# Loading the first tile of a rotary-embedding kernel in halves on two queues, with the tables behind one half

## The chip, the cores and the metric

The kernel runs on one core of a Trainium2 chip. Its time is the device time of one execution in microseconds, as the median of several; the span of a profile is shorter by some 1.4 us (161.19 against 159.8 in the profiled run of the kernel before). Runs of the kernel before agree within about 0.5%; a few runs come out some per cent slower, and comparisons leave those out.

## The reference

`x` is 16 x 512 x 1024 in float32, that is 33.6 MB in and as much out. Each row of 1024 is 16 heads of 64, and each head is rotated by tables that depend on the position alone:

```
x1, x2 = x[..., :32], x[..., 32:]                 # per head
rotated = concatenate([x1*cos - x2*sin, x1*sin + x2*cos])
```

`cos` and `sin` are 512 x 32 each: 64 KB, and so each about a thousandth of the bytes moved.

## The kernel before

The data are cut into 10 tiles. Tiles 0, 1, 8 and 9 hold one batch (4 rows of 1024 per partition, 2 MB); the six between hold two batches (8 rows, 4 MB). They live in a ring of 40 rows, so the first six tiles can be loaded at once; the other four are loaded when stores have freed their place. For each of the 64 rows VectorE writes x times cosine to PSUM, and GpSimd writes the swapped x times the signed sine to one of six buffers in SBUF (six of the rows have this product on VectorE). The sum is made by VectorE for 43 rows, and for 21 by TensorE, which adds the second product into PSUM; ScalarE then copies the result back.

ScalarE issues all the loads, in one queue, with both tables behind tile 0. SyncE issues all the stores.

```python
def on_scalar(ae):
    later = {}
    for t, (b, n) in enumerate(tiles):
        if b * R1 + n <= RING:
            load(ae, t)                                # tiles 0 to 5
        else:
            later.setdefault(... + R2 - 1 + LAG, []).append(t)
        if t == 0:
            for i, (table, sem) in enumerate(((cos, sem_cos), (sin, sem_sin))):
                ae.dma_start(stage[:, i, :], table.rearrange("(s r) d -> s (r d)", r=R1)).then_inc(sem, 16)
    ae.wait_ge(sem_sin, 16)
    ...                                                # the signed sine tables
    for u in range(NU):
        if PE2[u]:                                     # TensorE's rows: copy the sum back
            ae.wait_ge(sem_e, n_pe[u])
            ae.activation(xs[:, u % RING, :], t1_ps[:, u % NT1, :], COPY).then_inc(sem_a, 1)
        for t in later.get(u, ()):                     # a reissued load waits for a store
            ...
            ae.wait_ge(sem_out[k], 16 * stores_of(k))
            load(ae, t)
```

GpSimd's program: it waits for the signed sine table before its first row (and for that of the larger tiles before tile 2, left out below), then per tile for its load, and per row for a free buffer.

```python
    for u in range(NU):
        ...
        if (t, r) == (0, 0):
            pl.wait_ge(sem_s, 1)
        ...
        pl.wait_ge(sem_in[t], 16)
        wait_t2_free(pl, u)
        pl.tensor_tensor(t2_sb[:, u % NT2, :, :, :], swapped(k), over_heads(s_of(t, r)), mult).then_inc(sem_p, 1)
```

## Time and profile before

| | before |
|---|---|
| time, median of 3 runs | 161.44 us |
| span of the profile | 159.8 us |
| bytes moved | 67.26 MB, at 421 GB/s over the span |
| DMA engines | busy from 1.83 us to 159.35 us |
| GpSimd | 58 products, 134.1 us busy, from 9.56 to 149.74 us |
| last add ends, last store issued | 151.06, 151.14 us |

Two things stand close to the end of this kernel: the bytes, and GpSimd. The prediction below shows the lines of the page. One more is needed here, from SyncE's own waits (columns: what waited for what, total in us, times, longest): the wait for the last store after it was issued.

```profile
SPq L162 <- DMA out_dram<-x_sb: 8.3, 1, 8.3
```

A store of 2 MB is 8 packets of 16 KB on each engine, of 0.611 us each in this trace, 4.9 us. That this one took 8.3 us from its issue shows that stores had piled up: the compute was finished before the queue was.

### The profile page before, as it was taken

What the parts mean: (1) busy time and instruction counts of PE and PEld (TensorE: products, weight loads), DVE (VectorE), ACT (ScalarE), POOL (GpSimd) and SP (SyncE); (2) the same over time, 40 slices, a digit from 0 to 9 for tenths busy, and PEclk for the clock granted to TensorE, in tenths of its full rate; (3) what the DMA queues carried; (4) which work ended last, traced back from release to release, by engine and by line L of the source; (5) the groups of instructions that cost most, each with busy time, mean ns of one, the idle gap of its engine ahead of it and who ended that gap; (6) DMA issues with size and microseconds to landing.
All of it is one profiled execution on the core that took longest, in us unless ns stands there. A gap on an engine that the chain in (4) does not pass through costs nothing.

```text
span 159.8 us, 568 instructions
## 1 busy us (share of the span) xinstructions
PE 70.9 (44%) x94; PEld 23.3 (15%) x94; DVE 130.6 (82%) x117; ACT 23.9 (15%) x26; POOL 136.4 (85%) x67
## 2 busy tenths in 40 slices
PE   6050005375437642680943409435848764950000
PEld 1020002021202210220211002110222121310000
DVE  0069998799999999987989729899989998989500
ACT  0320000205020502022012020222022202130000
POOL 5069999999999999999999999994999999289400
PEclk9999999959876995576598775995555555576555
DMA  5999999999999999999999999999999999999997
GB/s 144 395 458 480 394 394 431 422 509 410 394 427 427 494 418 402 451 459 404 402 468 443 394 459 451 402 435 418 418 439 472 435 402 418 492 402 435 390 447 304
DMA packets 3170, 67.26 MB, mean 421 GB/s; under 512 B 352, under 2 KB 608, under 8 KB 608
## 3 DMA queue, kind: packets, MB, share of 16 engines
q10 hardware_dynamic: 1728, 33.69, 49.8%
q1 hardware_dynamic: 1440, 33.56, 48.8%
q14 instruction: 2, 0.02, 0.0%
HBM read 33.69 MB, written 33.55 MB: 421 GB/s over the span
## 4 chain that ended last, share of the span: by engine, by line
DMA 30%; POOL 18%; issue 17%; DVE 17%; PE 8%; ACT 3%; ACTq 2%; POOLq 0%; DVEq 0%; SPq 0%
DMA out_dram<-x_sb 18%; POOL t_sb L265 18%; DMA x_sb<-in_x_dram 11%; DVE x_sb L312 8%; PE t_ps L220 8%; DVE t_ps L301 7%; ACT x_sb L186 3%; ACTq L153 1%; DVE t_sb L294 1%; ACTq L174 1%; POOLq L144 0%; POOLq L146 0%; DVEq L311 0%; DVEq L146 0%; SPq L137 0%
## 5 line engine op out<-in xcount | busy, mean ns | idle before, releaser
L265 POOL TENSOR_TENSOR t_sb<-x_sb,s_sb 128x1024 f32<-128x1024 f32 x58 | 134.1, 2363 | 12.5 <-ACT s_sb L178 6.5
L220 PE MATMUL t_ps<-t_sb,ident 128*128 128x512 f32 x84 | 66.1, 940 | 64.8 <-DVE t_ps L301 34.7
L301 DVE TENSOR_TENSOR t_ps<-x_sb,pair_ps 128x1024 f32<-128x1024 f32 x48 | 57.7, 1223 | 8.2 <-ACT x_sb L186 7.9
L312 DVE TENSOR_TENSOR x_sb<-t_ps,t_sb 128x1024 f32<-128x1024 f32 x43 | 52.4, 1220 | 2.7 <-POOL t_sb L265 2.6
L186 ACT ACTIVATE x_sb<-t_ps 128x1024 f32<-128x1024 f32 x21 | 21.5, 1023 | 109.8 <-PE t_ps L220 97.7
L220 PEld LDWEIGHTS t_ps<-t_sb,ident 128*128 128x128 f32 x84 | 21.4, 279 | 109.2 <-DVE t_ps L301 60.2
L301 DVE TENSOR_TENSOR t_ps<-x_sb,tab_ps 128x1024 f32<-128x1024 f32 x16 | 19.3, 1222 | 1.1 <-DMA x_sb<-in_x_dram 0.6
L294 DVE TENSOR_TENSOR t_sb<-x_sb,tab_ps 128x1024 f32<-128x1024 f32 x6 | 7.3, 1215 | 0.0
L272 DVE COPY tab_ps<-stage 128x128 f32<-128x128 f32 x1 | 0.3, 295 | 7.6 <-DMA stage<-in_cos_dram 7.6
L203 PE MATMUL pair_ps<-stage,pick 128*128 128x256 f32 x4 | 2.0, 668 | 5.1 <-DMA stage<-in_sin_dram 5.1
L196 PE MATMUL t_ps<-zero 128*128 128x512 bf16 x6 | 2.7, 630 | 1.3 <-DVE zero L270 1.3
L177 ACT ACT_TABLE_LOAD x1 | 1.3, 1283 | 5.4 <-issue 5.4
L203 PEld LDWEIGHTS pair_ps<-stage,pick 128*128 128x128 f32 x4 | 1.2, 326 | 6.1 <-issue 6.0
L246 POOL TENSOR_SCALAR_AFFINE_SELECT pick<-pick 128x128 f32<-128x128 f32 x2 | 1.4, 704 | 0.1
L196 PEld LDWEIGHTS t_ps<-zero 128*128 128x128 bf16 x6 | 0.7, 137 | 2.4 <-DVE zero L270 1.2
L270 DVE MEMSET zero<- 128x256 uint32 x1 | 0.3, 272 | 0.9 <-PEq L345 0.9
L177 ACT ACTIVATE s_sb<-stage 128x128 f32<-128x128 f32 x1 | 0.3, 310 | 2.3 <-DMA stage<-in_sin_dram 2.3
L181 ACT ACTIVATE s_sb<-pair_ps 128x256 f32<-128x256 f32 x1 | 0.4, 384 | 1.7 <-PE pair_ps L203 1.7
L231 POOL MEMSET ident<- 128x128 f32 x1 | 0.2, 205 | 0.3 <-POOLq L345 0.3
L182 ACT ACTIVATE s_sb<-pair_ps 128x256 f32<-128x256 f32 x1 | 0.4, 378 | 0.0
L233 POOL TENSOR_SCALAR_AFFINE_SELECT ident<-ident 128x128 f32<-128x128 f32 x1 | 0.3, 294 | 0.1
L345 POOL MEMSET const-float32-0.0<- 128x1 f32 x1 | 0.1, 98 | 0.3 <-issue 0.3
(7 smaller groups left out, 1.3 us busy)
## 6 DMA issues: line engine op xcount, KB each, us to landing
x_sb<-in_x_dram ACTq DMA_DIRECT2D x6, 4096.0 KB, 38.8
out_dram<-x_sb SPq DMA_DIRECT2D x6, 4096.0 KB, 25.7
x_sb<-in_x_dram ACTq DMA_DIRECT2D x4, 2048.0 KB, 22.7
out_dram<-x_sb SPq DMA_DIRECT2D x4, 2048.0 KB, 15.0
stage<-in_cos_dram ACTq DMA_DIRECT2D x1, 64.0 KB, 7.5
stage<-in_sin_dram ACTq DMA_DIRECT2D x1, 64.0 KB, 7.3
```

What stands on the lines that cost most here:

```text
L153: eng.dma_start(in_sbuf(t), in_dram(x1, x2, t)).then_inc(sem_in[t], 16)
L174: ae.dma_start(stage[:, i, :], table.rearrange("(s r) d -> s (r d)", r=R1)).then_inc(sem, 16)
L177: ae.activation(s1_sb[:, :, 0, :], sv, COPY, scale=-1.0)
L186: ae.activation(xs[:, u % RING, :], t1_ps[:, u % NT1, :], COPY).then_inc(sem_a, 1)
L196: pe.matmul(t1_ps[:, k, b * BANK:(b + 1) * BANK], zero[:, 0:P], zero[:], start=True, stop=True).then_inc(sem_w, 1)
L203: pe.matmul(pair_ps[:, k].rearrange("p c r d -> p (c r d)"), pick[:, k].rearrange("q s b -> q (s b)"), stage[:].rearrange("q c f -> q (c f)"),
L220: ins = pe.matmul(t1_ps[:, u % NT1, b * BANK:(b + 1) * BANK], ident[:], t2[:, b * BANK:(b + 1) * BANK], start=False, stop=True, skip_group ...
L246: pl.affine_select(out=pick[:, k], in_=pick[:, k], compare_op=mybir.AluOpType.is_equal, fill=0.0, base=-k, pattern=[[-2, P // 2], [0, 2]], ...
L265: pl.tensor_tensor(t2_sb[:, u % NT2, :, :, :], swapped(k), over_heads(s_of(t, r)), mult).then_inc(sem_p, 1)
L294: ve.tensor_tensor(t2_sb[:, u % NT2, :, :, :], swapped(k), over_heads(v_ps), mult)
L301: ve.tensor_tensor(t1_ps[:, u % NT1, :].rearrange("p (h d) -> p h d", d=HALF), x_sb[:, k, :, :, :].rearrange("p h t d -> p (h t) d"), c_of ...
L312: ve.tensor_tensor(xs[:, k, :], t1_ps[:, u % NT1, :], t2_sb[:, u % NT2, :, :, :].rearrange("p h t d -> p (h t d)"), add,).then_inc(sem_v, 1)
```

## The change

Two queues are to start at once, so that the first tile should be there sooner, and the tables should come right behind it without standing before tile 1. The core of the diff; the waits for tile 0 count 32 in place of 16, as the tile now has two DMAs with `then_inc(sem_in[0], 16)`:

```diff
+        def load_half(eng, i):
+            eng.dma_start(
+                x_sb[:, i * HR:(i + 1) * HR].rearrange("p n h t d -> p (n h t d)"),
+                x1[0, :, i * HR * dim:(i + 1) * HR * dim],
+            ).then_inc(sem_in[0], 16)
 ...
         def on_sync(sp):
+            load_half(sp, 0)
+            for i, (table, sem) in enumerate(((cos, sem_cos), (sin, sem_sin))):
+                sp.dma_start(stage[:, i, :], table.rearrange("(s r) d -> s (r d)", r=R1)).then_inc(sem, 16)
 ...
         def on_scalar(ae):
+            load_half(ae, 1)
             later = {}
             for t, (b, n) in enumerate(tiles):
+                if t == 0:
+                    continue
                 if b * R1 + n <= RING:
                     load(ae, t)
 ...
-                if t == 0:
-                    for i, (table, sem) in enumerate(((cos, sem_cos), (sin, sem_sin))):
-                        ae.dma_start(stage[:, i, :], ...).then_inc(sem, 16)
```

More of the change, by code (lines that the diff above doesn't have):

```diff
@@ L150, in stores_of @@
             return sum(b * R1 // R2 == k for b, _ in tiles)
+        HR = R1 // 2
+        def load_half(eng, i):
[3 more added lines that the diff above has]
+            ).then_inc(sem_in[0], 16)
         def load(eng, t):
@@ L171, in on_scalar @@
                     later.setdefault((b * R1 - RING) // R2 * R2 + R2 - 1 + LAG, []).append(t)
-                if t == 0:
-                    for i, (table, sem) in enumerate(((cos, sem_cos), (sin, sem_sin))):
-                        ae.dma_start(stage[:, i, :], table.rearrange("(s r) d -> s (r d)", r=R1)).then_inc(sem, 16)
             ae.wait_ge(sem_sin, 16)
@@ L262, in on_gpsimd @@
                     pl.wait_ge(sem_s, 2)
-                pl.wait_ge(sem_in[t], 16)
+                pl.wait_ge(sem_in[t], 32 if t == 0 else 16)
                 wait_t2_free(pl, u)
@@ L286, in mul @@
                 if r == 0:
-                    ve.wait_ge(sem_in[t], 16)
+                    ve.wait_ge(sem_in[t], 32 if t == 0 else 16)
                 if (t, r) == (2, 0):
```

## The prediction

> **What bounds the kernel now.** I read the page's slices first, then the queue totals, the groups, the windows, the chain, the timeline of the start, and last the single packets of the DMA record.
>
> ```profile
> span 159.8 us, 568 instructions
> ...
> DMA  5999999999999999999999999999999999999997
> ...
> DMA packets 3170, 67.26 MB, mean 421 GB/s; under 512 B 352, under 2 KB 608, under 8 KB 608
> ...
> q10 hardware_dynamic: 1728, 33.69, 49.8%
> q1 hardware_dynamic: 1440, 33.56, 48.8%
> ```
>
> The 16 DMA engines are busy from the first slice to the last. q10 is ScalarE's queue (all loads), q1 SyncE's (all stores). The packet record gives 611 ns for a 16 KB packet and 1213 ns for a 32 KB one on one engine, so 16 engines move 429 to 432 GB/s and 67.2 MB need about 156 us. The kernel is bound by its bytes. What stands beside them is GpSimd:
>
> ```profile
> L265 POOL TENSOR_TENSOR t_sb<-x_sb,s_sb 128x1024 f32<-128x1024 f32 x58 | 134.1, 2363 | 12.5 <-ACT s_sb L178 6.5
> ...
> L272 DVE COPY tab_ps<-stage 128x128 f32<-128x128 f32 x1 | 0.3, 295 | 7.6 <-DMA stage<-in_cos_dram 7.6
> ```
>
> 58 products occupy it 134.1 us, 2.31 us from one to the next. It is idle 12.5 us: 6.5 before the first, until the sine table is there, and 6.0 after. Of those 6.0, the waits give 5.8 to loads:
>
> ```profile
> POOL t_sb L265 <- ACT s_sb L178: 6.5, 1, 6.5
> POOL t_sb L265 <- DMA x_sb<-in_x_dram: 5.8, 2, 3.6
> ```
>
> So a later start of GpSimd is free only for about 6 us; after that GpSimd sets the end. The start, from the timeline:
>
> ```profile
> 1.21 0.46 ACTq L174 DMA_DIRECT2D stage<-in_cos_dram  x1
> 1.69 0.45 ACTq L174 DMA_DIRECT2D stage<-in_sin_dram  x1
> ...
> 8.97 0.31 ACT L177 ACTIVATE s_sb<-stage 128x128 f32<-128x128 f32 x1 [2.25 <-DMA stage<-in_sin_dram]
> ...
> 9.56 20.80 POOL L265 TENSOR_TENSOR t_sb<-x_sb,s_sb 128x1024 f32<-128x1024 f32 x9 [6.50 <-ACT s_sb L178]
> ```
>
> Sine lands just before 8.97, and 0.59 us later GpSimd starts. The end, from the chain in order of time and the windows (columns PE, PEld, DVE, ACT, POOL, clock, DMA share, GB/s):
>
> ```profile
> 149.84 1.23 DVE x_sb L312
> ```
>
> ```profile
> 150.00:160.00 10.00, 0.00 (x0) 0.00 (x0) 1.06 (x1) 0.00 (x0) 0.00 (x0) 0.50 0.88 377
> ```
>
> The last add ends at 151.07, its store is issued at 151.14, but its first packets run at 153.7 to 154.5, behind the previous store; the last packet ends at about 159.3. Compute has some 2.7 us of slack even there.
>
> [...] q1 and q10 together never exceed the rate of one alone. [...] From 24 us to 37.5 us one engine's packets run store 16 KB, load 32 KB, store 16 KB, load 32 KB, one of each, for all eight of a DMA, whatever their size. At 37.47 us even the 4-byte packets that end each DMA [...] take turns: load's 4 B, store's 4 B (6 ns later), load's 32 KB. So here a turn is one descriptor, however small. [...]
>
> **The change part by part.** (1) First tile in halves on two queues. Bytes are equal; both halves start with the first packet at about 1.83 us as before (ScalarE issues at 0.81, SyncE is free as early). An engine does 16 packets of 8 KB in turns in place of 8 of 16 KB; by the 16 KB and 32 KB times a packet costs some 9 ns beside its bytes, so 8 x 9 = 0.07 us more. Both halves land where the tile landed, about 7.65 to 7.9 us. Issue time saved is worth nothing, as the first packets come 1.0 us after the issue's start anyway. Worth: 0, at most 0.3 us either way.
>
> (2) Tables behind their half on SyncE's queue. Before, they stood in ScalarE's queue between tile 0 and tile 1; an engine did its 8 + 8 packets of 512 B in 16 x 27 ns = 0.43 us with nothing between. After, SyncE's ring holds 8 packets of cosine and 8 of sine, and ScalarE's ring holds tile 1 (8 x 16 KB per engine), then tile 2 (8 x 32 KB). One for one, cosine goes beside tile 1: 8 x (0.611 + 0.027) = 5.1 us. Sine goes beside tile 2: 8 x (1.213 + 0.027) = 9.9 us. So sine ends at 7.9 + 5.1 + 9.9 = 22.9 us, as tile 2 ends; in the trace of before tile 2 ends at 22.6 to 23.1, with the same bytes ahead of it, which checks the sum. With 0.45 us from last packet to the waiting engine, as before (8.53 to 8.97), and perhaps one 32 KB packet less if the table goes first in each pair: sine lands at 22.3 to 23.5, say 23.0, in place of 8.97. That is 14.0 us later.
>
> (3) What follows. GpSimd starts at 23.6 in place of 9.56. Loads run on meanwhile and fill the 40-row ring; DMA loses no time at first, but stores begin 14 us later, at about 34 us. GpSimd then should find its inputs there: the ring holds the first six tiles, and the later loads, reissued when stores land, come 14 us later than before at worst while their use is as much later. I count its two load waits (3.64 + 2.16) as gone. Its end: 149.75 + 14.0 - 5.8 = 157.95. The last add, 1.32 later: 159.3. Then the last store without a backlog: stores before it are done, since 4.9 us of the previous 2 MB fit into the 9 us between the two. Issue to first packet 1.0 us (0.81 to 1.83 above), 8 x 0.611 = 4.9, plus 0.3 for engines that start late and 0.45 from last packet to the end of the span: 159.35 + 1.0 + 4.9 + 0.3 + 0.45 = 166.0 us of span. Kernel time is 161.44 - 159.8 = 1.64 above the span: 167.6 us. The stores alone give the same bound: the next-to-last pair's store is issued at about 143 to 146, then 9.7 + 4.9 + 4.9 us of packets: 163.5 to 166.5.
>
> **The rivals.** *Tables land early.* If an engine takes all eight 512 B descriptors in one turn [...], the tables wait for two or three big packets and land at 9 to 11 us. GpSimd loses at most 2 us, the 6 us of waits absorb that, and the bytes set the end again: 161.0 to 161.8. Against it: the 4-byte packets that take single turns, and each 512 B descriptor a packet of its own in the record (608 packets under 2 KB = 352 + 256 table packets). Chance 0.13. *Late tables, and more lost behind.* With GpSimd never waiting, VectorE has 64 + 43 + 6 operations of 1.22 us less overlap, about 130 us, to fit beside its 134, and TensorE's adds in the windows run at a granted clock of 0.50 to 0.67. If they hold VectorE up, or the later stores delay the reissued loads, 1 to 3 us come on top: 168.5 to 170.5. For it: VectorE waits 8.3 us for ScalarE's copies of TensorE's sums now. Against it: GpSimd waited only 0.3 us for TensorE. Chance 0.2. *Partly late:* only cosine is late[...]: start 6 to 8 us later, 162.5 to 164.5. Chance 0.07. *Faster:* from halves landing sooner. The bytes forbid it: 0.01.
>
> **Range and chances.** 0.6 for the main sum at 165.5 to 168.5, 0.2 above it, 0.2 below. Predicted 167.6; 165.0 to 169.8 should hold it 8 times in 10. Slower by 2% begins at 164.7: faster 0.01, same 0.14, slower 0.85.
>
> **What would show it.** Right: GpSimd's idle before its first product near 20 us, with the sine table as releaser; the issue-to-landing time of cosine near 12 and of sine near 21 to 22 us against 7.5 and 7.3; no wait of GpSimd for loads later; DMA slices below 9 late in the span; 2.31 us per product unchanged. Wrong: tables landing before 12 us with the time at 161 (turns are not single descriptors), or tables landing at 23 and the time below 165 (more slack in GpSimd than the 6 us I counted), or GpSimd still waiting for loads.

The sum came to 166.0 us of span and 167.6 us of time. The record's "descriptor" is one packet of the trace (the page's 608 packets under 2 KB are 352 of 4 B and 256 of 512 B, the rows of the two tables), and its "ring" is the packets of one queue on one engine. That the two queues together are no faster than one is seen in the windows of the kernel before: 431 GB/s from 8 to 24 us with loads alone, 436 and 434 GB/s from 30 to 60 and from 60 to 100 us with loads and stores. The 0.3 us "for engines that start late" was an estimate; in the changed kernel the 16 engines started the last store within 0.15 us (161.035 to 161.186).

## The result, and the profile after

The changed kernel takes 167.66 us (median of 6 runs, 167.52 to 167.97), the kernel before in the same rounds 161.43 us. The ratio is 1.0391, with a 95% interval of 1.0377 to 1.0405. Here and below a ratio is the mean time of one kernel's fast runs over that of the other's in the same rounds, so it is not quite the ratio of the medians.

The issues and landings of the changed kernel (columns: what is written and read, engine, how many, size of each, us from issue to landing):

```profile
x_sb<-in_x_dram SPq DMA_DIRECT2D x1, 1024.0 KB, 7.4
x_sb<-in_x_dram ACTq DMA_DIRECT2D x1, 1024.0 KB, 8.4
stage<-in_cos_dram SPq DMA_DIRECT2D x1, 64.0 KB, 12.9
stage<-in_sin_dram SPq DMA_DIRECT2D x1, 64.0 KB, 22.4
```

Both tables took 7.3 to 7.5 us before. The sine table, 64 KB, now takes three times as long as half a tile of 1 MB. The timeline of the start shows who stands waiting, and the waits show what GpSimd waits for in the whole run:

```profile
14.20 0.29 DVE L284 COPY tab_ps<-stage 128x128 f32<-128x128 f32 x1 [13.00 <-DMA stage<-in_cos_dram]
...
24.14 0.31 ACT L189 ACTIVATE s_sb<-stage 128x128 f32<-128x128 f32 x1 [18.51 <-DMA stage<-in_sin_dram]
```

```profile
POOL t_sb L277 <- ACT s_sb L190: 21.6, 1, 21.6
```

```profile
L277 POOL TENSOR_TENSOR t_sb<-x_sb,s_sb 128x1024 f32<-128x1024 f32 x58 | 134.1, 2375 | 21.6 <-ACT s_sb L190 21.6
```

GpSimd starts at 24.73 us in place of 9.56 and then never waits again: its whole idle time, 21.6 us, is that one wait. The two waits for loads, 5.8 us before, are gone from the list. It is busy 134.1 us, as before.

The DMA row of the page (tenths of busy time in 40 slices), SyncE's wait for the last store, and two windows of the changed kernel (columns: us, busy time and count of PE, PEld, DVE, ACT, POOL, granted clock, DMA share, GB/s):

```profile
DMA  5999999998999988989898989999998999489887
```

```profile
SPq L174 <- DMA out_dram<-x_sb: 6.0, 1, 6.0
```

```profile
72.00:84.00 12.00, 7.13 (x8) 2.35 (x8) 11.59 (x11) 1.29 (x2) 12.00 (x6) 0.57 0.93 358
139.00:150.00 11.00, 7.86 (x9) 2.68 (x10) 10.59 (x10) 1.67 (x2) 11.00 (x6) 0.50 0.76 325
```

The DMA engines now have holes while GpSimd fills both windows (12.00 of 12.00, 11.00 of 11.00 us): the bound has passed from the bytes to GpSimd. And the last store no longer stands in a queue.

The ledger, from the two traces:

| | before | after | difference |
|---|---|---|---|
| GpSimd's first product | 9.56 | 24.73 | +15.17 |
| its idle time after that | 6.0 | 0 | -6.0 |
| its last product ends | 149.74 | 158.80 | +9.06 |
| last add ends | 151.06 | 160.13 | +9.07 |
| from there to the last packet's end | 8.29 | 6.00 | -2.29 |
| last packet ends | 159.35 | 166.13 | +6.78 |

Why the table is late is seen in the single packets of the trace. A table is 128 rows of 512 B, and each row is one packet there (256 packets of 512 B for the two), eight on each of the 16 engines. Behind a DMA's last packet on an engine there is one of 4 B (352 in the kernel before, 16 for each of its 22 DMAs). This is one of the engines in the changed kernel, from where the first tile's halves end (queue 1 is SyncE's, 10 ScalarE's; a part). The trace does not name a packet's engine; I joined each packet to the one that starts where it ends:

```
start us   queue  bytes   ns
  7.602      1      512    27     cosine, 1st of 8
  7.625     10    16384   611     tile 1
  8.232      1      512    27
  8.256     10    16384   611
   ...
 12.016      1      512    27     cosine, 8th
 12.039     10    16384   611
 12.647      1        4     9     cosine's 4 B packet
 12.652     10        4     9     tile 1's 4 B packet
 12.658      1      512    27     sine, 1st of 8
 12.682     10    32768  1213     tile 2
 13.891      1      512    27
 13.915     10    32768  1213
   ...
 21.299      1      512    27     sine, 8th
 21.323     10    32768  1219
 22.538      1        4     9     sine's 4 B packet
```

The two queues alternate here, one packet each: behind each of the 256 packets of 512 B a packet of ScalarE's loads starts within 4 ns of its end. 4 KB of sine on this engine take 9.9 us, of which 0.22 us (8 x 27 ns) are the table's own.

### The profile page after: what moved, and what is told of

The parts are those of the page before. It is cut to its first block, busy times and chain, and to the rows that moved or that the text cites. A ratio compares the mean times of both kernels' runs of the same rounds, so it can differ in the third digit from the quotient of the medians.

```text
span 166.6 us, 569 instructions
## 1 busy us (share of the span) xinstructions
PE 70.1 (42%) x94; PEld 22.9 (14%) x94; DVE 130.1 (78%) x117; ACT 24.0 (14%) x26; POOL 136.4 (82%) x67
## 4 chain that ended last, share of the span: by engine, by line
DMA 29%; POOL 23%; DVE 16%; PE 12%; issue 11%; ACT 3%; ACTq 1%; SPq 0%; DVEq 0%; POOLq 0%
POOL t_sb L277 23%; DMA out_dram<-x_sb 15%; DMA stage<-in_sin_dram 13%; PE t_ps L232 12%; DVE t_ps L313 8%; DVE x_sb L324 6%; ACT x_sb L198 3%; DVE t_sb L306 1%; ACTq L162 1%; SPq L167 0%; SPq L156 0%; ACT s_sb L189 0%; ACT s_sb L190 0%; DVEq L323 0%; POOLq L146 0%
## 5 line engine op out<-in xcount | busy, mean ns | idle before, releaser
L277 POOL TENSOR_TENSOR t_sb<-x_sb,s_sb 128x1024 f32<-128x1024 f32 x58 | 134.1, 2375 | 21.6 <-ACT s_sb L190 21.6
L232 PE MATMUL t_ps<-t_sb,ident 128*128 128x512 f32 x84 | 65.3, 925 | 60.9 <-DVE t_ps L313 46.9
```

Source lines behind the costliest of these rows:

```text
L232: ins = pe.matmul(t1_ps[:, u % NT1, b * BANK:(b + 1) * BANK], ident[:], t2[:, b * BANK:(b + 1) * BANK], start=False, stop=True, skip_group ...
```

## The experiments

The theory: (a) as in the packets above, the tables and the loads take turns on an engine one packet at a time, so a table's time is its number of packets times the packet beside it; (b) GpSimd's start can slip for free as far as its load waits and the backlog of stores reach, and sets the end beyond that. The main rivals: the halves or the second queue cost by themselves (lost bandwidth), the second queue is merely served late whatever stands beside it, or any delay of the start is paid in full. Times are medians; ratios are to the kernel before in the same rounds.

### The halves without the tables

The changed kernel, with the tables in ScalarE's queue again, behind its half.

```diff
 def on_sync(sp):
     load_half(sp, 0)
-    for i, (table, sem) in ...: sp.dma_start(stage[:, i, :], ...)
 def on_scalar(ae):
     load_half(ae, 1)
+    for i, (table, sem) in ...: ae.dma_start(stage[:, i, :], ...)
```

> Tile 0 in halves on both queues as in the change, but both tables in ScalarE's queue behind its half, ahead of tile 1. Theory (the tables' single-descriptor turns beside big loads): sine has only SyncE's first-half packets of 8 KB beside it and lands near 9 us, GpSimd starts near 9.6, time 161.2 to 161.7. Rival (splitting the tile over two queues itself costs, or costs bandwidth): 164 to 168.

Measured: 161.19 us (161.11 to 161.20), ratio 0.9993 (0.9977 to 1.0009). The start is the old one:

```profile
9.75 27.74 POOL L277 TENSOR_TENSOR t_sb<-x_sb,s_sb 128x1024 f32<-128x1024 f32 x12 [6.68 <-ACT s_sb L190]
```

So the halves cost nothing and bring nothing, 9.75 against 9.56 us at GpSimd's start. All of the 6 us belongs to the tables' place.

### The lateness without halves and without a second queue

The kernel before, with one number changed: the tables stand behind tile 2 in ScalarE's only load queue.

```diff
-                if t == 0:
+                if t == 2:
                     for i, (table, sem) in enumerate(((cos, sem_cos), (sin, sem_sin))):
```

> The kernel before with nothing changed but the place of the tables in ScalarE's one queue: behind tile 2 in place of behind tile 0; no halves, no second queue. Theory (only the sine table's lateness costs): sine lands at 23.6 to 24.0, GpSimd starts near 24.3, waits for no load later, time 166.8 to 167.8, as the changed kernel. Rival (two queues side by side, or halves, cost by themselves): clearly under 167, near 161.4 to 164.

Measured: 167.51 us (167.50 to 167.73), ratio 1.0389. The same lateness, with no sharing at all, gives the changed kernel's time. The group of the products has the same form as in the changed kernel, with all idle time in one wait:

```profile
L265 POOL TENSOR_TENSOR t_sb<-x_sb,s_sb 128x1024 f32<-128x1024 f32 x58 | 134.0, 2376 | 21.2 <-ACT s_sb L178 21.2
```

Cosine and sine are both late here, at 23.5 and 23.7 us, and the time is the same as with cosine at 14.2: of the two, sine's arrival sets it.

### A small delay: tables alone on SyncE's queue, and tables behind tile 1

In one kernel tile 0 stays whole and the tables alone go to SyncE's queue. In the other the kernel before has its tables behind tile 1 (`if t == 1`).

```diff
 def on_sync(sp):
+    for i, (table, sem) in enumerate(((cos, sem_cos), (sin, sem_sin))):
+        sp.dma_start(stage[:, i, :], table.rearrange("(s r) d -> s (r d)", r=R1)).then_inc(sem, 16)
 ...                                                    # the same lines go from on_scalar
```

> Tile 0 whole on ScalarE's queue; only the tables move to SyncE's queue, with nothing ahead of them. Theory (one turn each): cosine's 8 turns go beside tile 0's 8 packets and land near 8.6, sine's 8 beside tile 1's 16 KB packets (5.1 us) and land near 13.7; GpSimd starts near 14.3, 4.7 us late, inside its slack (6.0 us of load waits and some 2.7 of store backlog at the end), so time 161.2 to 161.9. Rival (any lateness of GpSimd is paid in full): 165.9 to 166.2. Rival (eight small descriptors go in one turn): sine lands below 5 us.

> The kernel before with the tables behind tile 1 in ScalarE's one queue. Sine lands near 13.9, GpSimd starts near 14.5, 4.9 us later than before. Slack theory (free up to a start of about 18.4 us): 161.2 to 161.9. Rival (paid in full): 166.3.

Measured: 161.80 us (161.36 to 161.90), ratio 1.0027 (1.0004 to 1.0050), for the tables alone; GpSimd starts at 12.87 us. 161.93 us (161.67 to 162.32), ratio 1.0042 (1.0021 to 1.0063), for the tables behind tile 1; it starts at 14.58. Delays of 3.3 and 5.0 us cost 0.4 and 0.7 us in the mean, where payment in full would have cost all of it. The slack is real, though not quite free, as both intervals lie above 1. Both traces point at where the 0.4 and 0.7 us come from: GpSimd's last product ends at 148.74 and 149.00 us, but the last add only at 153.81 and 153.90, some 5 us later (1.3 in the kernel before), and ScalarE waited far longer for stores to land (3.4 us before), first for the tables alone, then for the tables behind tile 1:

```profile
ACT x_sb L185 <- DMA out_dram<-x_sb: 11.6, 2, 6.3
ACT x_sb L186 <- DMA out_dram<-x_sb: 11.3, 2, 7.1
```

The small-partner kernel below shows the same wait, and there it was tested; in these two it was not.

In the first of the two I had cosine near 8.6 us and sine at 13.7. VectorE's copy of cosine ran at 7.16 us and ScalarE's of sine at 12.28, so both landed some 1.5 us sooner than one turn each would have it. Why was not shown.

### Twice the packets, the same bytes

The changed kernel, with sine loaded in two halves of its columns: 16 pieces of 256 B per engine in place of 8 of 512 B (the edit in part).

```diff
+            HT = R1 * HALF // 2
+            for i in range(2):
+                sp.dma_start(stage[:, 1, i * HT:(i + 1) * HT],
+                             sin.rearrange("(s r) d -> s (r d)", r=R1)[:, i * HT:(i + 1) * HT]).then_inc(sem_sin, 16)
 ...
-            ae.wait_ge(sem_sin, 16)
+            ae.wait_ge(sem_sin, 32)                    # TensorE's wait likewise
```

> The changed kernel with the sine table loaded in two column halves: the same bytes, but 16 descriptors of 256 B per engine in place of 8 of 512 B. Theory (a turn is one descriptor, whatever its size): the second eight go beside tile 3's 32 KB packets, sine lands 9.7 us later, near 33.8, GpSimd starts near 34.4, time 176.8 to 177.8. Rival (turns count bytes, or several small descriptors go in one turn, or the table waits for a fixed amount of loads): sine near 24 to 25, time 167.5 to 168.5.

Measured: 177.40 us (177.27 to 177.55), ratio 1.0996. The timeline:

```profile
33.47 0.31 ACT L194 ACTIVATE s_sb<-stage 128x128 f32<-128x128 f32 x1 [27.73 <-DMA stage<-in_sin_dram]
...
34.06 2.34 POOL L282 TENSOR_TENSOR t_sb<-x_sb,s_sb 128x1024 f32<-128x1024 f32 x1 [30.99 <-ACT s_sb L195]
```

GpSimd starts at 34.06 us, 9.33 later than in the changed kernel, and the time is 9.7 us longer. Eight more pieces on each engine, beside tile 3's 32 KB packets of 1.213 us (9.7 us for eight), cost about those eight packets' time, with not a byte more to move. So in this run the delay went with the number of pieces and not with the bytes.

### Small packets beside the table

The changed kernel, with tile 2, whose packets stand beside the sine table, loaded in four pieces of 2 rows (8 KB packets in place of 32 KB; the edit in part, the waits for tile 2 count 64).

```diff
         def load(eng, t):
+            if t == 2:
+                for j in range(n // HR):
+                    eng.dma_start(x_sb[:, k:k + HR]..., x2[:, b:b + 2, j * HR * dim:(j + 1) * HR * dim]).then_inc(sem_in[t], 16)
+                return
```

> The changed kernel with tile 2 loaded in four pieces of 2 rows, so that the packets beside the sine table are of 8 KB (0.309 us) in place of 32 KB (1.213 us). Theory: sine's 8 turns take 2.7 us in place of 9.9, sine lands near 17, GpSimd starts near 17.6, just inside the slack that ends at a start of about 18.4; time 161.3 to 162.3. Rival (the partner's size does not matter, the second queue is served late): sine near 24, time 167.6.

Measured: 163.13 us (162.14 to 163.31), ratio 1.0096 (1.0062 to 1.0130). The mechanism came out as written:

```profile
17.05 20.80 POOL L286 TENSOR_TENSOR t_sb<-x_sb,s_sb 128x1024 f32<-128x1024 f32 x9 [13.99 <-ACT s_sb L199]
```

GpSimd starts at 17.05 us, 7.68 us sooner than in the changed kernel, because the packet beside the table is a quarter as large (in the changed kernel an 8 KB packet took 309 ns, one of 32 KB 1213). The time did not: it is about 1 us above what I had written. Two waits of the profiled run (162.14 us, the fastest of the four) point at the cause:

```profile
ACT x_sb L207 <- DMA out_dram<-x_sb: 10.0, 2, 6.7
DVE t_ps L322 <- ACT x_sb L207: 6.5, 6, 3.2
```

ScalarE's program has a reissued load between two of its copies. It stands before a store that is later now (10.0 us in all, 3.4 in the kernel before), and VectorE stands behind it for want of a free PSUM buffer. These waits only point: VectorE's was longer in the kernel before (8.3 us in all), where it cost nothing that shows. GpSimd's last product ends at 151.04 us, but the last add at 154.19.

### Is that the missing microsecond?

Three kernels: the one above with the reissued loads three rows later in ScalarE's program; the kernel before with the four pieces of tile 2 alone; the kernel before with the later reissue alone.

```diff
-    LAG = 10
+    LAG = 13
```

> The kernel with the small partner packets, which came out at 163.1 us where 161.3 to 162.3 was expected, and the reissued loads three rows later in ScalarE's program (LAG 13 in place of 10). Theory: the extra 1 us came from ScalarE standing before a store's landing (10.0 us of waits there) while VectorE needed its copies; three rows later the wait is nearly gone (under 3 us) and the time is 161.3 to 162.3. Rival (the four small loads, or GpSimd's late start itself, cost it): 163.0 again.

> Control: the kernel before with tile 2 loaded in four pieces of 2 rows, the tables where they were. If the four small loads cost nothing: 161.2 to 161.7. If they are the extra of the small-partner kernel: 162.5 to 163.3.

> Control: the kernel before with LAG 13 in place of 10. The queue of loads never runs dry, and the bytes set the end, so 161.1 to 161.8; ScalarE's wait for a store (3.4 us before) goes. If a later reissue starves the loads: above 162.

Measured: 161.56 us (161.41 to 162.14), ratio 1.0017 (0.9995 to 1.0038), with both. ScalarE's wait for the stores is no longer in the list of waits, and the last add ends at 152.57 us. The four pieces alone take 161.31 us, ratio 0.9995. The later reissue alone takes 161.13 to 161.53 us in five timed runs, ratio 0.9995; its profiled execution was an outlier of 301.88 us in which ScalarE waited 251.3 us for TensorE (97.7 in the kernel before), so its trace says nothing about an ordinary run, and whether its 3.4 us wait went is not seen. What made TensorE slow in that one execution I do not know.

So the extra goes with ScalarE's wait (the edit also moves the four loads themselves, which is not told apart), and with it removed GpSimd's start at 17.01 us, 7.45 us late, costs no more than 0.4%. Neither edit is an improvement of its own: both controls, put into the kernel before, leave its time where it was.

### The tables in the other order

The changed kernel, sine ahead of cosine on SyncE's queue.

```diff
-            for i, (table, sem) in enumerate(((cos, sem_cos), (sin, sem_sin))):
+            for i, (table, sem) in ((1, (sin, sem_sin)), (0, (cos, sem_cos))):
```

> The changed kernel with the two tables in the other order on SyncE's queue. Theory: sine lands near 14.1 and GpSimd starts near 14.8; cosine lands near 24 and VectorE starts its products there in place of at 14.5. GpSimd runs six buffers ahead and then waits for VectorE, which has 130 us of work left from 24.4 and some stalls: time 163.5 to 166.5, between the two kernels, with VectorE and not GpSimd setting the end. Rival (only GpSimd's start matters): 161.4. Rival (it is the later of the two tables that counts, in full): 167.6.

Measured: 164.30 us (163.33 to 164.96), ratio 1.0176 (1.0133 to 1.0218): slower, but not clearly by 2%. In the profiled run, the fastest of the four, GpSimd starts at 14.41 us, VectorE's copy of cosine runs at 23.75, and then:

```profile
POOL t_sb L277 <- PE t_ps L232: 2.8, 3, 2.0
```

GpSimd's last product ends at 151.36 us and the last add 4.0 us later, at 155.39 (1.3 us in the changed kernel): VectorE, whose first product starts at 24.08 us in place of 14.53, is the one behind. Of the three outcomes only the middle one fits. A late table costs by the engine that it holds up, and VectorE had more slack than GpSimd.

### All together

| kernel | GpSimd starts | time, us | time minus start |
|---|---|---|---|
| before | 9.56 | 161.43 | |
| halves only | 9.75 | 161.19 | |
| tables alone on SyncE's queue | 12.87 | 161.80 | |
| one queue, tables behind tile 1 | 14.58 | 161.93 | |
| small partner, later reissue | 17.01 | 161.56 | |
| small partner | 17.05 | 163.13 | |
| one queue, tables behind tile 2 | 24.30 | 167.51 | 143.2 |
| the change | 24.73 | 167.66 | 142.9 |
| twice the packets | 34.06 | 177.40 | 143.3 |

Where GpSimd sets the end, the time is its start plus 143 us. That line meets the 161.4 us of the bytes at a start of 18.3 us: below it the delay is nearly free (but for ScalarE's wait in the small-partner kernel), above it every microsecond is paid. No kernel starts between 17.05 and 24.30 us, so the corner at 18.3 us is worked out and not measured. The kernel with sine first is left out: there VectorE sets the end, 2.9 us late at a GpSimd start of 14.41. None of the kernels beats the kernel before beyond its noise.

## Why the prediction was right

**The bound.** The bytes held the kernel before, with GpSimd close behind. Right: its DMA row has no slice below 9 between the first and the last, starts of GpSimd 3.3 and 5.0 us later cost 0.4 and 0.7 us, and the row gets holes only once GpSimd starts late enough.

**Part 1, the halves: worth nothing, 0.07 us more in packets.** Right. An 8 KB packet took 309 ns, two of them 7 ns more than one of 16 KB (I had worked out 9), and the halves alone gave a ratio of 0.9993.

**Part 2, one packet a turn.** Right, and this was the step that carried the forecast. Cosine's eight turns were to take 5.1 us and took 5.05 (7.602 to 12.647 on the engine shown); sine's eight were to take 9.9 and took 9.88 (12.658 to 22.538). The landing was 1.1 us later than the 23.0 us I settled on. I had allowed for one big packet less if the table goes first in each pair. It did go first, but on the engine shown the table's 4 B packet ran at 22.538 us, as the eighth big packet ended. And the slowest engine ended its half of tile 0 at 8.6 us, not 7.9, and ran sine's 4 B packet at 23.58. The 7.65 to 7.9 us for the tile's landing was a misreading: in the kernel before, too, the slowest engine ran the tile's 4 B packet at 8.09 us.

**Part 3, the slack and the sum.** The 14.0 us of delay became 15.2, and the two load waits went, as counted. GpSimd ended at 158.80 us for the 157.95 forecast, and the profiled span is 166.6 us for 166.0. The time still agrees to 0.1 us, and part of that is luck: I added 1.64 us from the span to the time, a median less a single span, where the profiled runs show 1.4, and that made up some of what sine's landing had lost. (The profiled run is also the slowest of the six; the spans of the others are 166.1 to 166.3 us.) The 6 us of slack in GpSimd's load waits was right. The 2.7 us read as slack at the end were somewhat too many, as they hold the microsecond or so that a store takes from issue to first packet without a backlog too (0.8 us in the changed kernel). With the 2.29 us of the ledger, which the sum took in through the last store, the free stretch is 8.3 us by the ledger, and 8.7 us by the meeting point at 18.3 us.

**What I had not seen.** That "DMA loses no time at first" held to about 60 us. No load ran from 60.1 to 73.5 us, since the six tiles of the ring were in and ScalarE issued the next load at 67.97 us. Stores filled most of this, but between two of them all 16 engines stood empty from 62.55 to 63.33 us. And twice a queue that had just been given work was not served at once: the load issued at 67.97 us first ran at 73.53, after the eight 32 KB packets of the store that had the engines, and the first store, issued at 35.36 beside running loads, first ran at 38.94, where the last store, with the engines empty, took 0.8 us from issue to first packet (160.20 to 161.03). One packet each is thus shown only for the tables and the loads of this trace from 7.6 to 23.6 us, and for loads and stores in the kernel before, from 24 to 37.5 us; what a newcomer waits for was not tested.

**The rivals.** Tables in one turn: excluded by the doubled packets. Partly late: excluded by sine's landing at 24.1 us. Faster through the halves: excluded by the halves alone. More lost behind a late start, with VectorE held up: it did not happen in the changed kernel, where GpSimd never waited, but it is real in between, at a start near 17 us, through ScalarE's reissued loads and not through TensorE's clock, which I had suspected: the extra went while the mean granted clock of the profiled runs was 0.79 with it and 0.74 without. The 0.50 to 0.67 that I gave for the clock were also only some of the windows; between 30 and 60 us they show 0.82 and 0.83.

## What to carry to other kernels

Before moving a small transfer to another queue, count its pieces per DMA engine and look at what will stand beside them: here each cost one packet of the other queue, and 64 KB in 512 B pieces, eight per engine, took 9.9 us beside 32 KB packets (1.213 us each). Here the table that everything waits for was best placed in the loads' own queue right behind the first tile, where its packets ran back to back (27 ns each, 16 on an engine in 0.43 us); ahead of the first tile was not tried. And before paying for a start that slips, or for one that comes sooner, add up the waits that would absorb it: here the first 8 us were nearly free, and as the bytes set the end, nothing was to be expected from a sooner start.
